# Seven products in every w2 step, sums that stay in PSUM over a pass boundary, and the residual parked in DRAM

## The chip, the cores and the metric

The kernel runs on one core of one Trainium2 chip. The metric is device time in microseconds: the median of three runs of the kernel before is 1998.59 (1996.66 to 1999.63). The engines are named as in the profile: TensorE is PE (its weight loads PEld), VectorE is DVE, ScalarE is ACT, SyncE is SP, whose queue issues nearly all DMA transfers.

## The reference

256 positions of 2048 channels go through two layers, everything in float32. Layer 0 mixes by a gated short convolution, layer 1 by latent attention with 16 heads; each mixer is followed by a squared-ReLU feed-forward part of 8192 hidden channels, and each of these four sub-layers by a layer norm of `ALPHA * x + f(x)`.

```python
def short_conv_mixer(x, w_in, conv_w, w_out):
    gate_b, gate_c, u = jnp.split(x @ w_in, 3, axis=-1)
    y = conv3(gate_c * u, conv_w)              # causal, width 3, per channel
    return (gate_b * y) @ w_out

def sq_relu_mlp(x, w1, w2):
    return jnp.square(jax.nn.relu(x @ w1)) @ w2

# layer 0: mix = short_conv_mixer(h); layer 1: mix = mla_mixer(h)
h = layer_norm(ALPHA * h + mix, ...)
h = layer_norm(ALPHA * h + sq_relu_mlp(h, w1, w2), ...)
```

## The kernel before

**Arithmetic.** Every float32 operand is split into a rounded part `hi` and a rest `lo` (`split`, L125: ScalarE casts, VectorE subtracts), and a product is three matmuls: hi·hi, hi·lo, lo·hi. Weights are split on the chip as they arrive.

**The weight stream.** `stream` (L78) lists all weight blocks of 128 × 1024 in the order of use. `take` (L183) hands out the next block and runs `prepare` (L141) for blocks up to `LOOK` = 5 steps ahead: a load on SP's queue into one of `RAW` = 5 raw buffers, the cast by ScalarE and the subtraction by VectorE into one of `WA` = 8 pairs of hi and lo tiles. A raw buffer is free when VectorE has read it, a hi or lo tile when TensorE has. The compiler's scheduler puts the instructions of each engine into one fixed order, which may differ from the order of the Python text; at run time each engine goes through its list in that order and waits for semaphores.

**The feed-forward part** (`mlp`, L575) is used twice, as part 1 after the convolution (profile from about 362 to 1057 us) and as part 3 after the attention (from about 1304 us on). It goes through eight passes q over 1024 hidden channels each (eight chunks of 128). In a pass the w1 products come first: eight chunks m, each 32 matmuls of TensorE (`products`, L288), evacuated by `whole` (L352; ScalarE copies a half, VectorE adds), then relu and square on ScalarE (`hidden`, L713). Then come the w2 products.

**Passes 1 to 6** (`FAST`) use Strassen-like sums for w2. Positions are cut into two halves, the 2048 output columns into four blocks of 512, two column blocks making a group g. For a pair j of hidden chunks and a group, seven products of 128 × 512 (`FACTORS`, L340) replace eight. They need sums S1 to S4 of the activations (`form`, L703, into the tile `forms`) and differences T1 to T4 of the weights, made by VectorE in three steps of `prepare`: block r1 is split; T1 and T3 are computed and split; T2 and T4 are computed and split with r2. `MIXED = "sssp"` says that in the first group (g = 1) three pairs go by seven products and the fourth ("p") by the eight plain dots; the second group (g = 0) takes seven products for all four pairs. One plain matmul is cut into two halves (`EVEN`).

**Sums.** Each of the seven products, and an eighth bank for the plain pair, is summed over pairs in a PSUM bank and over passes in SBUF: in `sums` (for products 1, 5, 7 and 6) or in `acc`. `resumed` copies a sum into its bank (ScalarE), `put_back` copies it out (ScalarE), `keep` adds it to what lies in SBUF (VectorE). `fold` (L669) makes the output blocks out of the sums in pass 7. Four banks serve the w1 products, four hold sums.

**The residual** lies in `xres` (2 MB) all the time. In part 1 `begin` runs `Norm.prepare` on its 16 chunks, chunk 0 in pass 0 and the others in pass 7. In part 3 `extra` (`turn_residual`, L1024) transposes it on TensorE and adds it into `acc`, a quarter in each of the passes 1 to 4.

Of the kernel before, what the change touches and what calls it, by code (L numbers as in the profile page):

```python
# [16 lines left out]
P = 128  # L17
W = 256 + 2
T = 256
# [14 lines left out]
RAW, WA = 5, 8  # L34
# [3 lines left out]
MIXED = "sssp"  # L38
EVEN = (QC - 1, "22")
# [7 lines left out]
WO_G = 3  # L47
BEHIND = (2, 2, 2, 3, 2, 2, 3)
# [5 lines left out]
def trunk(ctx: ExitStack, tc: tile.TileContext, xT, vecs, lead, w_first, w_in, w_out, w_kv, w_q, w_uk, w_uv,  # L54
# [12 lines left out]
    xres = act.tile([P, NC, T], F32, tag="xres", name="xres")  # L67
    for tag, columns in (("c", 4096), ("a2", 4128), ("a1", 4128), ("b", 8256)):
        act.tile([P, columns], F32, tag=tag, name=f"at_{tag}")
# [7 lines left out]

    stream = []  # L78
# [20 lines left out]
    stream += halves(w_o) + mlp_stream(1)  # L99

# [40 lines left out]
    def prepare(i):  # L141
# [7 lines left out]
        r1, r2 = (load_raw(f"{i}_{j}", src) for j, src in enumerate(stream[i]))  # L149
        out = []  # L150

        def finished(r, name):
# [3 lines left out]

        b22, (b21, b12) = r1[:, BW:], (r2[:, :BW], r2[:, BW:])
# [12 lines left out]
        f = state["fast"].tile([P, 2, BW], F32R, tag="t4", name=f"t4_{i}", bufs=2)  # L170
        split(f[:, 0, :], f[:, 1, :], t4)
        b1, t13, b2 = ([[v.rearrange("p b c -> p (b c)")[:, o:o + BW] for v in w] for o in (0, BW)] for w in out)
        ready[i] = {"11": b1[0], "22": b1[1], "21": b2[0], "T2": b2[1], "T1": t13[0], "T3": t13[1],
                    "T4": [f[:, 0, :], f[:, 1, :]]}
# [168 lines left out]
    def fast_products(ps, x, forms, j, fresh, ready, onto=()):  # L343

        b, = take(1)
        a = {"11": held(x[2 * j], 0), "12": held(x[2 * j + 1], 0), "22": held(x[2 * j + 1], 1)}
        for i in range(4):
            a[f"S{i + 1}"] = [forms[:, j, o, i * P:(i + 1) * P] for o in range(2)]
        for p, l, r in FACTORS:
            dot(ps[p], b[r], a[l], p in fresh, p in ready, onto=p in onto)  # L350

# [40 lines left out]
    class Norm:  # L392
# [10 lines left out]
        def prepare(self, m, bank=None):  # L403

            d = xres[:, m, :]
# [11 lines left out]
        def count(self, m):  # L417
            d = xres[:, m, :]
# [21 lines left out]
        def wide(self, m):  # L440
            d, x, g = xres[:, m, :], self.xd[m], self.gain(m)[0]
# [31 lines left out]
        def normal(self, m, dst=None):  # L473

            g, b = self.gain(m)
            d = xres[:, m, :]
# [22 lines left out]
    def add(ps, m):  # L499
        d = xres[:, m, :]  # L500
        nc.vector.tensor_tensor(d, d, ps[:, :T], ALU.add)

    def summed(ln, pss, add, m0=0):

        for m, ps in enumerate(pss, m0):
            add(ps, m)
            ln.count(m)
            ln.wide(m)
# [38 lines left out]
    ln = Norm(0, ALPHA)  # L547
    for m in range(NC):
# [19 lines left out]
        if m >= NC // 2:  # L568
            for k in range(2 * m - NC, 2 * m - NC + 2):
                ln.prepare(k)  # L570
    nc.sync.dma_start(id_t, ident)
    ln.widen("a1", "a2")
    summed(ln, chain(products(1, z), lagged(NC - 1, z)), residual)

    def mlp(idx, ln, blocks, fast, begin=None, extra=None, last=False):  # L575
# [25 lines left out]
        sums = fast.tile([P, 4, 2, BW], F32, name=f"sums{idx}")  # L601

        def place(p, g):

            return sums[:, OWN.index(p), g, :] if p in OWN else \
                block(*{"2": (2 * g, 0), "3": (2 * g + 1, 0), "4": (2 * g, 1), "22": (2 * g + 1, 1)}[p])

        def resumed(p, g, name, bank):

            ps = psum(name, bank)  # L610
            if q != FAST[0] or p not in OWN:
# [3 lines left out]
        def put_back(p, g, ps):  # L615
            nc.scalar.copy(place(p, g), ps)

        def keep(p, g, ps):

            at = place(p, g)  # L620
            if q == FAST[0] and p in OWN:
# [4 lines left out]
        def resume(busy, free, ps, m):  # L626

            b2, b3, b4, b6 = free
            b1, b5, b7, b22 = busy
            for p, bank in {3: (("3", b3),), 4: (("2", b2),), 5: (("4", b4), ("1", b1)), 6: (("6", b6), ("5", b5)),  # L630
                            7: (("7", b7), ("22", b22))}.get(m, ()):
                ps[p] = resumed(p, 1, f"ps_r{p}", bank)

        def down_pairs(h, forms, busy, free, ps):

            b2, b3, b4, b6 = free
            b1, b5, b7, b22 = busy
            new = set(OWN) if q == FAST[0] else set()
            onto = set(ps) - new
            for j, kind in enumerate(MIXED):  # L640
                if kind == "s":
                    last = j == MIXED.rindex("s")
                    fast_products(ps, h, forms, j, new if j == 0 else (), OWN if last else (), onto)
                    if last:
                        for p in OWN:
                            put_back(p, 1, ps[p])
                        then = {p: resumed(p, 0, f"ps_f{p}", bank) for p, bank in (("3", b1), ("1", b5))}
                    continue
                for two in (((0, "2"), (1, "4")), ((1, "22"), (0, "3"))):
                    w, = take(1, LOOK + 1)  # L650
                    for t, p in two:
                        for kk in range(2):
                            k = 2 * j + kk
                            dot(ps[p], wide_rows(w, kk), held(h[k], t), False, k == QC - 1, (k, p) == EVEN, True)
                    if j == len(MIXED) - 1:
                        if "5" not in then:
                            then.update({p: resumed(p, 0, f"ps_f{p}", bank) for p, bank in (("5", b7), ("7", b6))})
                        for _, p in two:
                            put_back(p, 1, ps[p])
            n = QC // 2  # L660
            onto = set(then) - new
            then.update({p: psum(f"ps_f{p}", bank) for p, bank in (("2", b2), ("6", b4), ("4", b22))})
            for j in range(n):
                fast_products(then, h, forms, j, set(then) - onto if j == 0 else (), then if j == n - 1 else (), onto)
            for p, _, _ in FACTORS:
                (put_back if p in onto or p in new else keep)(p, 0, then[p])
            return (b3, b1, b5, b7), (b6, b2, b4, b22)

        def fold():  # L669
# [3 lines left out]
            for d, a, b in ((c[:, 0, 0], c[:, 0, 0], s1), (s6, s6, s1), (c[:, 0, 1], c[:, 0, 1], s6), (s7, s7, s6),  # L673
                            (c[:, 1, 0], c[:, 1, 0], s7), (c[:, 1, 1], c[:, 1, 1], s7),
                            (c[:, 0, 1], c[:, 0, 1], s5), (c[:, 1, 1], c[:, 1, 1], s5)):
# [10 lines left out]
        busy, free = (0, 1, 2, 3), (4, 5, 6, 7)  # L686
        for q in range(NQ):
            ht = act.tile([P, QC, 2 * T], F32R, tag="c", name=f"h{idx}_{q}")
            h = [ht[:, k, :] for k in range(QC)]
            forms = None  # L690
# [497 lines left out]
```

## Time and profile before

| | us |
|---|---|
| median of three runs | 1998.59 (1996.66 to 1999.63) |
| span of the profiled execution | 1994.9 |
| what lies between that span and the median | 3.7 |
| PE busy | 1987.7 (100% of the span) |
| PEld busy | 1737.2 (87%) |
| DVE busy | 1709.4 (86%) |
| ACT busy | 1354.9 (68%) |
| one pass of part 1, for example 619.23 to 702.46 | 83.23 |

Of the profiled execution the span, from its first to its last instruction, is what the profile gives as its own time. Matmuls are pipelined: the busy time of one (0.39 us at 512 columns) overlaps the next, so a busy PE is no proof that it never waits; the distance from start to start tells more. The same holds on a smaller scale for DVE. The granted TensorE clock is 1.00 throughout, so no stretch is slowed by the clock.

### The profile page before, as it was taken

The page shows a single profiled execution, that of the slowest core. Times are in us where ns is not written, and L with a number is a line of the kernel's source. Part 1 is how long each engine was busy: PE and PEld are TensorE (multiplying, and loading weights), DVE is VectorE, ACT ScalarE, POOL GpSimd, SP SyncE. Part 2 cuts the span into 40 slices and gives each one's busy share as a digit, 9 for nine tenths or more (in the row PEclk, how much of TensorE's full clock was granted, in tenths as well). Part 3 has the DMA queues.
Part 4 walks back from the last instruction along what each step waited for, and adds up shares of the span by engine and source line. Part 5 has one row for each costly group of instructions (what it writes and reads, how often), then busy time and mean ns, then how long its engine had stood idle before and what let it go on. Part 6 is the DMA issues. An engine that isn't in the chain of part 4 may idle for free.

```text
span 1994.9 us, 30180 instructions
## 1 busy us (share of the span) xinstructions
PE 1987.7 (100%) x11110; PEld 1737.2 (87%) x11110; DVE 1709.4 (86%) x2555; ACT 1354.9 (68%) x2154; POOL 2.3 (0%) x21
## 2 busy tenths in 40 slices
PE   9999999999999999999999999999999999999998
PEld 8888888988888888888889998898888888888886
DVE  8667667797999989989978988777899999999985
ACT  6444445586778778777756755558677787887772
POOL 0000000000000000000000000000000000000000
PEclk9999999999999999999999999999999999999999
DMA  8666666565657466574855543656464656656483
GB/s 318 205 191 187 190 190 190 179 193 157 212 170 251 148 216 221 177 243 147 281 171 159 170 140 123 201 180 195 146 233 155 232 161 220 222 178 233 150 269 130
DMA packets 106853, 385.85 MB, mean 193 GB/s; under 512 B 11857, under 2 KB 12625, under 8 KB 106449
## 3 DMA queue, kind: packets, MB, share of 16 engines
q1 hardware_dynamic: 106560, 383.79, 59.5%
q8 instruction: 87, 1.43, 0.3%
q14 instruction: 62, 0.50, 0.1%
q10 hardware_dynamic: 144, 0.13, 0.0%
HBM read 381.78 MB, written 2.10 MB: 192 GB/s over the span
## 4 chain that ended last, share of the span: by engine, by line
PE 98%; DVE 1%; ACT 1%; issue 0%; DVEq 0%; ACTq 0%
PE ps_u L215 20%; PE ps_l L215 13%; PE ps_u L219 10%; PE ps_l L219 7%; PE ps_f L300 4%; PE ps_f L303 4%; PE ps_f L302 4%; PE ps_r L303 4%; PE ps_r L302 4%; PE ps_r L300 4%; PE ps_d L300 2%; PE ps_d L302 2%; PE ps_d L303 2%; PE ps_w L249 2%; PE ps_w L248 2%; PE ps_w L247 2%
## 5 line engine op out<-in xcount | busy, mean ns | idle before, releaser
L128 DVE TENSOR_TENSOR lo<-raw,hi 128x1024 fp32r<-128x1024 f32 x710 | 861.8, 1220 | 190.6 <-ACT hi L127 119.9
L127 ACT CAST hi<-raw 128x1024 fp32r<-128x1024 f32 x710 | 741.8, 1051 | 247.4 <-PE ps_l L215 98.1
L215 PE MATMUL ps_u<-xhl,hi 128*128 128x512 f32 x1792 | 621.7, 392 | 0.0
L219 PE MATMUL ps_u<-xhl,lo 128*128 128x256 f32 x1792 | 498.2, 279 | 0.0
L215 PEld LDWEIGHTS ps_u<-xhl,hi 128*128 128x128 f32 x1792 | 334.5, 187 | 73.6 <-ACT acc L595 0.2
L219 PEld LDWEIGHTS ps_u<-xhl,lo 128*128 128x128 f32 x1792 | 338.1, 189 | 1.8
L215 PE MATMUL ps_l<-xhl_a,hi 128*128 128x512 f32 x704 | 244.1, 393 | 0.0
L219 PE MATMUL ps_l<-xhl_a,lo 128*128 128x256 f32 x704 | 195.4, 279 | 0.0
L215 PEld LDWEIGHTS ps_l<-xhl_a,hi 128*128 128x128 f32 x704 | 132.1, 188 | 29.9
L219 PEld LDWEIGHTS ps_l<-xhl_a,lo 128*128 128x128 f32 x704 | 131.9, 188 | 0.2
L127 ACT CAST hi_t<-raw_t 128x1024 fp32r<-128x1024 f32 x84 | 88.5, 1054 | 45.8 <-DVE raw_t L162 41.4
L162 DVE TENSOR_TENSOR raw_t<-raw,raw 128x1024 f32<-128x1024 f32 x84 | 102.3, 1218 | 1.8 <-DMA raw<-in_w2f_dram 1.5
L128 DVE TENSOR_TENSOR lo_t<-raw_t,hi_t 128x1024 fp32r<-128x1024 f32 x84 | 102.4, 1219 | 0.2
L718 ACT ACTIVATE fp<-fp 128x256 f32<-128x256 f32 x96 | 40.0, 416 | 63.2 <-DVE fp L356 62.6
L215 PE MATMUL ps_l<-z,hi 128*128 128x512 f32 x240 | 82.4, 391 | 0.0
L300 PE MATMUL ps_d<-hi,h 128*128 128x512 f32 x192 | 75.0, 391 | 0.0
L302 PE MATMUL ps_d<-lo,h 128*128 128x512 f32 x192 | 75.0, 390 | 0.0
L303 PE MATMUL ps_d<-hi,h 128*128 128x512 f32 x192 | 74.8, 389 | 0.0
L249 PE MATMUL ps_w<-xd,hi 128*128 128x258 f32 x256 | 72.7, 284 | 0.0
L248 PE MATMUL ps_w<-xd,lo 128*128 128x258 f32 x256 | 72.3, 282 | 0.0
L247 PE MATMUL ps_w<-xd,hi 128*128 128x258 f32 x256 | 72.3, 282 | 0.0
L215 PE MATMUL ps_l<-oT,hi 128*128 128x512 f32 x208 | 71.3, 391 | 0.0
(296 smaller groups left out, 3963.7 us busy)
## 6 DMA issues: line engine op xcount, KB each, us to landing
raw<-in_w_dram SPq DMA_DIRECT2D x344, 512.0 KB, 4.5
raw<-in_w2f_dram SPq DMA_DIRECT2D x168, 512.0 KB, 3.9
raw<-in_w_in_dram SPq DMA_DIRECT2D x88, 512.0 KB, 4.2
raw<-in_w_out_dram SPq DMA_DIRECT2D x32, 512.0 KB, 3.7
raw<-in_w_o_dram SPq DMA_DIRECT2D x32, 512.0 KB, 4.2
raw<-in_w_kv_dram SPq DMA_DIRECT2D x10, 512.0 KB, 3.7
raw<-in_w_q_dram SPq DMA_DIRECT2D x8, 512.0 KB, 4.0
raw<-in_w_uk_dram SPq DMA_DIRECT2D x8, 512.0 KB, 3.9
```

Of the source, the lines that this page charges most:

```text
L127: nc.scalar.copy(hi, src)
L128: nc.vector.tensor_tensor(lo, src, hi.bitcast(F32), ALU.subtract)
L162: nc.vector.tensor_tensor(t.rearrange(two, a=2), b12.unsqueeze(1).to_broadcast([P, 2, BW]), r1.rearrange(two, a=2), ALU.subtract)
L215: nc.tensor.matmul(ps, w[blk // 8][0][:, blk % 8, :], x, start=first, stop=False)
L219: nc.tensor.matmul(ps[:, :T], w[blk // 8][1][:, blk % 8, :], x[:, :T], start=False, stop=last)
L247: nc.tensor.matmul(ps[:, :W], hi, x[k][:, :W], start=k == 0, stop=False)
L248: nc.tensor.matmul(ps[:, :W], lo, x[k][:, :W], start=False, stop=False)
L249: nc.tensor.matmul(ps[:, :W], hi, x[k][:, W:], start=False, stop=k == NC - 1)
L300: nc.tensor.matmul(ps, x[0], w[0], start=first, stop=False, skip_group_check=onto)
L302: nc.tensor.matmul(ps[:, at], x[0], w[1][:, at], start=False, stop=False, skip_group_check=onto)
L303: nc.tensor.matmul(ps, x[1], w[0], start=False, stop=last, skip_group_check=onto)
L718: nc.scalar.activation(f, f, AF.Relu)
```

## The change

It has five parts.

1. **Seven products throughout.** `MIXED` and `EVEN` go. Both groups take seven products for all four pairs of a pass.
2. **Alternating groups.** Pass 1 takes the groups in the order (1, 0), pass 2 (0, 1), and so on, so that the last group of a pass is the first of the next. The sums of the products 3, 1, 5 and 7 of that group stay in their banks over the w1 products of the next pass (`stay`); the sums of 2, 6 and 4 are copied out at the end and in again in the next pass (`first_sums`). At the change of groups, in the last pair of the first group, each product's sum is copied out as soon as its last matmul is done and the next product's sum of the other group is copied into its bank (`turn`, called through `then`). All of these copies are ScalarE's; VectorE's additions (`keep` into SBUF) go.
3. **The residual in DRAM.** In part 1 `begin` runs in pass 1 for all chunks, each two chunks are stored to `parked` by SP's queue, and `sums` takes over the place of `xres`. In pass 7 four loads bring it back as `xback`. In part 3 `extra` turns all four quarters in pass 1.
4. **Deeper ring.** `RAW` goes from 5 to 7, `WA` from 8 to 9.
5. **One row.** Activations and sums of a pair lie in one row `u` of eight blocks of 128 columns: relu and square run once over 512 columns, three VectorE instructions instead of four make S1 to S4, and one split of 896 columns writes all seven left factors.

`EARLY` and `FRESH` are empty, so `making`, `made` and the branch of `prepare` for four sources do nothing here and are left out below.

```diff
-RAW, WA = 5, 8
+RAW, WA = 7, 9
-MIXED = "sssp"
-EVEN = (QC - 1, "22")
...
+    def groups(q):
+        return (1, 0) if (q - FAST[0]) % 2 == 0 else (0, 1)
...
-            for j, kind in enumerate(MIXED):
-                out += [(w2f[l, q, 1, j, 0], w2f[l, q, 1, j, 1])] if kind == "s" else \
-                    halves(w2[l, q, 2, j]) + halves(w2[l, q, 3, j])
-            out += [(w2f[l, q, 0, j, 0], w2f[l, q, 0, j, 1]) for j in range(QC // 2)]
+            for i, g in enumerate(groups(q)):
+                for j in range(QC // 2):
+                    out.append((w2f[l, q, g, j, 0], w2f[l, q, g, j, 1]) + made.get((l, q, i, j), ()))
...
+    LEFT = ("11", "22", "12", "S1", "S3", "S2", "S4")
+    def fast_products(ps, x, j, fresh, ready, onto=(), then=None):
         b, = take(1)
+        a = {n: [x[j // 2][:, j % 2, o, i * P:(i + 1) * P] for o in range(2)] for i, n in enumerate(LEFT)}
         for p, l, r in FACTORS:
             dot(ps[p], b[r], a[l], p in fresh, p in ready, onto=p in onto)
+            if then:
+                then(p)
...
+        def first_sums(ps, banks, m):
+            g = groups(q)[0]
+            for p in {3: ("3", "1", "5", "7") if q == FAST[0] else (), 4: "2", 5: "6", 6: "4"}.get(m, ()):
+                banks.setdefault(p, busy[m % 4])
+                ps[p] = begun_sum(p, g, f"ps_r{p}", banks[p])
...
+            def turn(p):
+                keep(p, first, ps[p], max(q - 1, FAST[0]) if p in order[:4] else q)
+                i = order.index(p) + 1
+                if i < len(order):
+                    begin_next(order[i], banks[p])
+            def end(p):
+                if p not in stay:
+                    keep(p, second, after[p], q)
...
+            for j in range(n):
+                if j == n - 1:
+                    begin_next(order[0], spare)
+                fast_products(ps, h, j, new - held_on if j == 0 else (), ps if j == n - 1 else (),
+                              set(ps) - (new - held_on), turn if j == n - 1 else None)
+            for j in range(n):
+                fast_products(after, h, j, new if j == 0 else (), after if j == n - 1 else (),
+                              set(order) - new, end if j == n - 1 else None)
...
+            def form(j, u):
+                a21, a11, a12, s1, s2, s4 = (u[:, i * P:(i + 1) * P] for i in (0, 1, 3, 4, 6, 7))
+                two = u.rearrange("p (i c) -> p i c", c=P)
+                nc.vector.tensor_tensor(s1, a21, u[:, 2 * P:3 * P], ALU.add)
+                nc.vector.tensor_tensor(two[:, 5:7, :], two[:, 0:5:4, :], a11.unsqueeze(1).to_broadcast([P, 2, P]),
+                                        ALU.subtract)
+                nc.vector.tensor_tensor(s4, a12, s2, ALU.subtract)
+                f = factors[j // 2][:, j % 2]
+                split(f[:, 0, :], f[:, 1, :], u[:, P:])
...
                 for m, ps in enumerate(products(QC, xhl, TURNED, busy)):
                     hidden(m, ps, whole)
-                    if extra and m == 0 and q <= NB:
+                    if extra and q == FAST[0] and m < NB:
                         for t in range(2):
-                            extra(block, q - 1, t, busy[2 + t])
+                            extra(block, m, t, busy[2 + t])
+                    if begin and q == FAST[0]:
+                        begin(range(max(2 * m, 1), 2 * m + 2))
+                        nc.sync.dma_start(parked[:, 2 * m:2 * m + 2, :], held_x[0][:, 2 * m:2 * m + 2, :])
+                    if q == FAST[0] and m == QC - 1:
+                        sums = act.tile([P, 4, 2, BW], F32, tag="xres", name=f"sums{idx}")
...
-                        if begin:
-                            begin(range(max(2 * m, 1), 2 * m + 2))
+                if begin and q == NQ - 1:
+                    held_x[0] = act.tile([P, NC, T], F32, tag="xres", name="xback")
+                    for k in range(0, NC, 4):
+                        nc.sync.dma_start(held_x[0][:, k:k + 4, :], parked[:, k:k + 4, :])
```

More of the change, by code (lines that the diff above doesn't have):

```diff
@@ L169, in prepare @@
         nc.vector.tensor_tensor(t4, b21, b12, ALU.subtract)
[L170 to L174, printed above, removed]
+        ready[i] = {**named((("11", "22"), ("T1", "T3"), ("21", "T2"))), "T4": fourth(t4)}
         yield
@@ L570, in trunk @@
                 ln.prepare(k)
+        if m >= MAKE_FROM:
+            next(before_mlp, None)
     nc.sync.dma_start(id_t, ident)
     ln.widen("a1", "a2")
-    summed(ln, chain(products(1, z), lagged(NC - 1, z)), residual)
+    summed(ln, chain(products(1, z), lagged(NC - 1, z)), residual, maker=before_mlp)
+    making_in.close()
     def mlp(idx, ln, blocks, fast, begin=None, extra=None, last=False):
@@ L710, in form @@
                 nc.vector.tensor_tensor(s4, a12, s2, ALU.subtract)
-                split(forms[:, j, 0, :], forms[:, j, 1, :], sf.rearrange("p i c -> p (i c)"))
+                f = factors[j // 2][:, j % 2]
+                split(f[:, 0, :], f[:, 1, :], u[:, P:])
             def hidden(m, ps, evac, *func):
-                both = pair_tile(m) if q in FAST else None
-                f = both[:, m % 2, :] if both is not None else tmp.tile([P, T], F32, tag="fh", name="fh", bufs=3)
+                if q in FAST:
+                    if m % 2 == 0:
+                        pair.append(fast.tile([P, 8 * P], F32, tag="fp", name="fp"))
+                    u = pair[-1]
+                    evac(ps, u[:, (m % 2) * T:(m % 2 + 1) * T])
+                    if m % 2:
+                        for function in (AF.Relu, AF.Square):
+                            nc.scalar.activation(u[:, :2 * T], u[:, :2 * T], function)
+                        form(m // 2, u)
+                    return
```

183 lines of the change are left out of this document (95 added, 88 removed).

## The prediction

> **What bounds the kernel now.** I read the page first, then stretches of one pass of the feed-forward part (tables of busy time by stretch), then the instructions at the end of a pass in order of time, and last the groups and waits of the engines that feed TensorE.
>
> ```profile
> span 1994.9 us, 30180 instructions
> PE 1987.7 (100%) x11110; PEld 1737.2 (87%) x11110; DVE 1709.4 (86%) x2555; ACT 1354.9 (68%) x2154; POOL 2.3 (0%) x21
> PE 98%; DVE 1%; ACT 1%; issue 0%; DVEq 0%; ACTq 0%
> ```
>
> By the page TensorE is the bound. The twelve fast passes (q = 1 to 6 of both feed-forward parts) show how near the next engine is. Columns: stretch in us, its length, then busy us of PE, PEld, DVE, ACT, POOL.
>
> ```profile
> 452.78:536.00 83.22, 83.22 (x429) 71.27 (x428) 72.44 (x96) 59.25 (x92) 0.00 (x0) 1.00 0.52 161
> 536.00:619.23 83.23, 83.23 (x429) 71.28 (x428) 78.12 (x101) 66.47 (x104) 0.00 (x0) 1.00 0.60 199
> 619.23:702.46 83.23, 83.23 (x430) 71.27 (x428) 80.16 (x104) 67.44 (x103) 0.00 (x0) 1.00 0.64 207
> 702.46:785.68 83.22, 83.22 (x429) 71.28 (x428) 78.12 (x101) 65.41 (x103) 0.00 (x0) 1.00 0.59 197
> 785.68:868.91 83.23, 83.23 (x429) 71.28 (x428) 79.66 (x104) 66.73 (x102) 0.00 (x0) 1.00 0.62 205
> 868.91:953.06 84.15, 83.69 (x429) 71.12 (x428) 78.52 (x102) 66.34 (x103) 0.00 (x0) 1.00 0.59 198
> 1394.56:1478.65 84.09, 84.09 (x438) 71.89 (x436) 73.90 (x98) 58.95 (x90) 0.00 (x0) 1.00 0.52 158
> 1478.65:1562.74 84.09, 84.09 (x437) 71.87 (x436) 79.64 (x104) 67.02 (x105) 0.00 (x0) 1.00 0.60 200
> ...
> 1814.15:1897.38 83.23, 83.23 (x429) 71.28 (x428) 78.53 (x101) 65.72 (x103) 0.00 (x0) 1.00 0.58 200
> 619.23:663.62 44.39, 44.39 (x257) 39.12 (x256) 41.67 (x58) 35.59 (x57) 0.00 (x0) 1.00 0.72 235
> 663.62:702.46 38.84, 38.84 (x175) 32.15 (x173) 38.49 (x47) 31.86 (x46) 0.00 (x0) 1.00 0.55 174
> ```
>
> A pass takes 83.23 us almost to the hundredth, so TensorE sets it; but VectorE is busy for 78.1 to 80.2 of it. The last two rows split one pass: 44.39 us of w1 products (VectorE 41.67 busy), then 38.84 us of w2 products, in which VectorE has no rest (38.49). It cannot keep up there and lives on weights prepared before. The end of that stretch shows what is left:
>
> ```profile
> 696.01 1.22 DVE L128 TENSOR_TENSOR lo_t<-raw_t,hi_t 128x1024 fp32r<-128x1024 f32 x1
> 697.15 1.22 DVE L128 TENSOR_TENSOR lo<-raw,hi 128x1024 fp32r<-128x1024 f32 x1
> 698.29 0.69 DVE L128 TENSOR_TENSOR t<-raw,t 128x512 fp32r<-128x512 f32 x1
> 698.89 2.35 DVE L128 TENSOR_TENSOR lo<-raw,hi 128x1024 fp32r<-128x1024 f32 x2
> ...
> 699.06 0.39 PE L300 MATMUL ps_f<-hi_t,forms 128*128 128x512 f32 x1
> 699.28 0.39 PE L302 MATMUL ps_f<-lo_t,forms 128*128 128x512 f32 x1
> 699.51 0.39 PE L303 MATMUL ps_f<-hi_t,forms 128*128 128x512 f32 x1
> ```
>
> The last pair's T1/T3 tile is done at 697.23 (696.01 + 1.22) and first read at 699.28: 2 us of reserve. Starts also give the true prices: 0.227 us per 512-column matmul (699.51 − 699.06, halved), 1.14 us per 1024-column VectorE instruction, 0.60 per 512-column one; the durations beside them overlap. The pass from 868.91 is 0.92 us longer than its fellows; in it the chain of waits runs through VectorE and ScalarE and ends with a sum copy that TensorE waits for:
>
> ```profile
> 936.91 0.52 ACT t L127
> 937.43 0.49 ACT acc L616
> 937.97 0.50 PE ps_f L300
> ```
>
> The Trainium skill (Perfetto Trace Analysis, Identifying the Most-Contended Engine) says matmul busy time does not tell the bound; weight-load busy time and the other engines' occupancy do. By it VectorE (99% of 663.62:702.46, weight loads 83%) is the contended engine of the second half, and TensorE time saved there would be worth nothing: VectorE's added 1.2 us a pass (below) would then be the whole effect, 10 × 1.2 = +12 us. The trace agrees half: 99% busy, yet no matmul late.
>
> **The change, part by part.**
>
> ```profile
> L128 DVE TENSOR_TENSOR lo<-raw,hi 128x1024 fp32r<-128x1024 f32 x33 | 40.1, 1220 | 2.5 <-ACT hi L127 2.3
> L162 DVE TENSOR_TENSOR raw_t<-raw,raw 128x1024 f32<-128x1024 f32 x7 | 8.5, 1218 | 0.2 <-DMA raw<-in_w2f_dram 0.2
> L166 DVE TENSOR_TENSOR raw<-raw,raw_t 128x512 f32<-128x512 f32 x7 | 4.8, 687 | 0.1
> L356 DVE TENSOR_TENSOR fp<-ps_u,t 128x256 f32<-128x256 f32 x8 | 3.3, 418 | 0.0
> L709 DVE TENSOR_TENSOR sf<-sf,fp 128x128 f32<-128x128 f32 x4 | 1.2, 291 | 0.1
> L624 DVE TENSOR_TENSOR acc<-acc,ps_f 128x512 f32<-128x512 f32 x3 | 2.0, 683 | 0.1
> ```
>
> (groups of the pass 619.23:702.46)
>
> *TensorE.* The one plain pair of a pass took 8 dots, 25 matmuls, one of them in two halves: 24 × 512 columns. A seven-product pair takes 21. Saved: 3 × 0.227 = 0.68 us a pass. A pass needs 82.55 us; if nothing stalls, 12 × 0.68 + 0.92 = 9.1 us are won. That is the ceiling, 1990.
>
> *VectorE.* A seven-product pair in place of the plain one adds one T1/T3 difference and one split (2 × 1.14 = 2.28) and three 512-column ones (1.8). Gone are the additions of L624 (34 in 12 passes, 2.8 × 0.60 = 1.7) and eight 512-column splits of h and forms (4.8); in their place four splits of 896 columns (between 0.60 and 1.14, taken as 1.00: 4.0). The four 128-column form instructions become two and one of 256; started back to back these are 0.08 shorter than 291 and 418 ns, so 8 × 0.2 less and 4 × 0.33 more: −0.3. Sum 2.28 + 1.8 − 1.7 − 4.8 + 4.0 − 0.3 = +1.3; from the compiled list +1.2, which I take. VectorE goes from 79.0 (mean of the six rows from 536.00 to 1562.74 that are not first passes) to 80.2 us, in 82.55.
>
> *The rings (RAW 7, WA 9).* A pair wants 4 × 1.14 + 3 × 0.60 = 6.4 us of VectorE and lasts 21 × 0.227 = 4.77 us. Eight pairs: 51 us against 38.2, so 13 must be ready ahead; before, 7 pairs and the plain one with the additions: 48.6 against 38.8, so 10. The ninth tile is worth about 2.1 us (a third of a pair). So the ring makes up most of the deficit, not all: reserve 2 − 1 = about 1 us at the best pass, none at others. The longer raw ring removes waits for loads, a part of the 2.5 us of idle time in the first row of groups.
>
> *ScalarE at the change of groups.* Before, eight sums were put back over a seven-product pair and the plain one:
>
> ```profile
> 674.74 0.59 ACT L616 COPY sums<-ps_r 128x512 f32<-128x512 f32 x1 [2.50 <-PE ps_r L303]
> 675.27 1.05 ACT L127 CAST hi_t<-raw_t 128x1024 fp32r<-128x1024 f32 x1
> 677.69 1.55 ACT L616 COPY sums<-ps_r 128x512 f32<-128x512 f32 x3
> 682.06 1.13 ACT L612 COPY ps_f<-sums 128x512 f32<-128x512 f32 x2
> ...
> ACT fp L718 <- DVE fp L356: 31.7, 28, 2.6
> ```
>
> Now one pair (4.77 us) ends all seven: 7 copies out and 6 in, 13 × 0.52 (674.74 to 675.27) = 6.8 us, with one cast between them in the compiled order. Casts behind them are late by 2 to 5 us, and VectorE's splits need the casts. Price: 0 (VectorE has other work) to 3 us a pass; I take 0.2 beyond the old waits, since the old order also held casts behind copies and VectorE still was 38.49 busy. The Trainium skill (TensorE: Matmul & The Clock Gate, Architectural detail) calls ScalarE and VectorE strict first-in, first-out. If so a cast can't pass the copies and the price is the upper end, 10 × 3 = 30 us; if casts could pass it is 0. The row of 674.74 (idle 2.50, the cast right behind) agrees, but shows no VectorE loss.
>
> Likewise relu and square now wait for both chunks of a pair, and one row is used in turn: ScalarE waited 31.7 us in 28 waits for VectorE there (L718, in the stretch 1400:1900). Fewer, later waits: −1 to +1 us a pass, taken as 0. In the compiled order VectorE prepares nine w1 tiles ahead of its work on the second chunk of a pass, where it prepared eleven: nine take 10.3 us, the two chunks 11.1 (44.39 / 4), so it may idle there for up to 1 us.
>
> *Banks over the pass boundary* save no copies (240 against 236 of ScalarE, and VectorE's 34 additions): 0.
>
> *The residual.* In the first part's pass 1: 16 prepare instructions (L415) come from pass 7, and eight 256 KB stores and four 512 KB loads go onto SP's queue.
>
> ```profile
> L415 DVE SCALAR_TENSOR_TENSOR xres<-xres,mu 128x256 f32<-128x256 f32 x45 | 16.6, 418 | 0.0
> SPq L138 <- DVE lo L128: 874.6, 368, 16.2
> out_dram<-acc SPq DMA_DIRECT2D x8, 256.0 KB, 2.4
> raw<-in_w_out_dram SPq DMA_DIRECT2D x32, 512.0 KB, 3.7
> ```
>
> 16 × 0.33 = 5.4 us of VectorE, in a pass with 10.8 idle (72.44 of 83.22): hidden. Behind a waiting store the next weight load waits; SP waits for VectorE's splits anyway (874.6 us). Without that cover it is 8 × 2.4 = 19 us, once. The loads go in pass 7 behind the last fold, 4 × 3.7 = 15 us if all in line, needed two column blocks (22 us) later: 0. In the second part the turning of the residual (84.09 − 83.23 = 0.86 us in each of four passes) moves into pass 1, 3.5 us in all; its banks are handed on at once, so TensorE may wait up to four times 1 us for VectorE: 1 us.
>
> **Sum.** Twelve passes before: 953.06 − 452.78 + 1897.38 − 1394.56 = 1003.1 us. After: first passes 82.55 and 82.55 + 3.5 + 1 = 87.0; the ten others as long as VectorE needs, 80.2 plus its idle time. That was 3.1 to 5.6 us before, mean 4.5 over the same six rows (5.11, 3.07, 5.11, 3.57, 5.63, 4.45). With 4.5 + 0.2: 84.9, but the deeper raw ring gives some of it back; I take 84.6, 0.3 less. 846 + 169.5 − 1003.1 = +12.4. The profiled span 1994.9 lies 3.7 below the median of 1998.59: 1994.9 + 12.4 + 3.7 = 2011.
>
> **Rivals.**
> - *The rings hide it.* VectorE's idle time falls to 2.3 to 2.8 us and a pass takes 82.55 to 83.0 us: 4 to 9 us won, 1990 to 1995. For it: idle time includes waits for a full ring, which cost nothing, and 3.07 was enough once. Against it: that pass kept only 2 us of reserve with a smaller deficit. Below 83.4 us a pass (833.6 + 169.5 = 1003.1) the kernel is faster than before.
> - *A tie.* Passes of 83.0 to 83.8: within 4 us.
> - *ScalarE's burst becomes the bound.* Each change of groups costs 3 us more: passes of 86 to 87.5, 2025 to 2040. For it: 6.8 us of copies in 4.77. Against: they end before TensorE needs the banks.
> - *Nothing is done.* Excluded: the list has 48 matmuls fewer.
>
> **How the numbers follow.** 0.2% is 4 us, what repeated runs can tell. Forecast (83.8 to 86 us a pass, 2003 to 2025) 0.58; burst 0.06; tie 0.12, rings 0.24. Range 1990 to 2025; the forecast's own is 2003 to 2025. Faster 0.24, same 0.12, slower 0.64.
>
> **What would show it.** Right: passes 2 to 6 of 84 us or more, VectorE above 80 us in each, and TensorE waiting for lo_t near the end of the second group; about 48 matmuls less; pass 1 near 82.6. Wrong: passes of 82.55 with VectorE idle 2 us. The weakest step is that VectorE's idle time stays as it was.

## The result and the profile after

The changed kernel takes 2022.62 us (median, 2022.02 to 2023.62); the kernel before, run beside it, 1998.57 (1996.66 to 1999.63). The ratio is 1.012 with a 95% interval of 1.0105 to 1.0134: slower by 24 us. The profiled execution has a span of 2021.0 us, 26.1 more than before.

The page of the changed kernel (span; busy time by engine; the chain that ended last, by engine):

```profile
span 2021.0 us, 29789 instructions
...
PE 2002.4 (99%) x11062; PEld 1726.4 (85%) x11062; DVE 1727.7 (85%) x2485; ACT 1332.7 (66%) x1998; POOL 2.3 (0%) x21
...
PE 73%; DVE 15%; ACT 8%; issue 5%; DMA 0%; DVEq 0%; ACTq 0%; SPq 0%
```

48 matmuls are gone, yet the span grew. The chain of waits was 98% TensorE's before; now 15% of it runs through VectorE and 8% through ScalarE. The stretches (columns as in the prediction: stretch, its length, then busy PE, PEld, DVE, ACT, POOL, clock, DMA share, GB/s) of both first passes, of the passes 2 to 6 of each part taken together, and of the two halves of one pass:

```profile
452.95:539.16 86.21, 84.46 (x426) 70.08 (x424) 72.29 (x89) 56.20 (x79) 0.00 (x0) 1.00 0.49 146
539.16:965.74 426.58, 421.88 (x2122) 351.48 (x2120) 403.21 (x482) 322.49 (x443) 0.00 (x0) 1.00 0.62 198
1409.30:1496.87 87.57, 87.11 (x458) 73.75 (x456) 77.16 (x97) 56.50 (x78) 0.00 (x0) 1.00 0.46 138
1496.87:1922.77 425.90, 421.10 (x2122) 351.16 (x2121) 403.31 (x482) 322.82 (x443) 0.00 (x0) 1.00 0.61 198
...
624.07:669.14 45.07, 45.07 (x256) 39.15 (x256) 41.58 (x52) 33.30 (x45) 0.00 (x0) 1.00 0.69 234
669.14:709.49 40.35, 39.40 (x171) 31.20 (x170) 39.01 (x46) 31.09 (x44) 0.00 (x0) 1.00 0.50 156
...
1753.33:1838.05 84.72, 83.76 (x425) 70.11 (x424) 80.67 (x97) 64.48 (x89) 0.00 (x0) 1.00 0.60 199
```

(the last row is a pass of part 3) and the passes 2 to 6 of the kernel before:

```profile
536.00:953.06 417.06, 416.61 (x2141) 356.22 (x2140) 394.58 (x508) 332.41 (x511) 0.00 (x0) 1.00 0.61 201
...
1478.65:1897.38 418.73, 418.73 (x2165) 358.17 (x2164) 397.39 (x514) 333.05 (x512) 0.00 (x0) 1.00 0.60 201
```

The ten passes went from 835.79 to 852.48 us (83.58 to 85.25 each), the two first passes from 167.31 to 173.78. That is 23.2 of the 26.1 us; the other 2.9 lie outside the twelve passes, 1.4 of them in the w1 products of the last pass of each part, 45.1 us each where 44.39 are needed. VectorE's work went from 79.20 to 80.65 us a pass and its idle time from 4.38 to 4.60.

These w1 products got slower without a wait on record and at a granted clock of 1.00, and so did those inside most passes: in 624.07:669.14 two of them (512 and 256 columns) follow the two before after 0.353 us (six such pairs from 639.83 to 641.95), where the kernel before needs 0.347 (639.70 to 641.78). Seven of the ten passes show it and take 85.41 to 85.63 us; the three that don't take 84.91, 84.72 and 84.72. So some 0.7 us of those seven passes, and of the two last w1 halves, is neither VectorE's work nor a wait that the trace names. In no_t4 and early_2 (below) none of the ten passes shows it. What causes it was not found.

Where the time goes is seen at the end of a pass. The chain of waits there (start, us, what):

```profile
779.55 1.10 ACT hi L159
...
780.68 0.04 DVE lo L160
...
788.25 1.15 DVE raw_t L216
...
789.42 0.02 ACT hi_t L159
789.44 0.93 issue
790.37 1.05 ACT hi L159
...
791.47 1.02 PE ps_f L350 x3
```

From 780.68 VectorE works without a break; the T1/T3 difference of the last pair is finished only at 789.40, ScalarE casts it and then the next block, and TensorE starts on that block 0.05 us after the cast. Nothing is ready ahead any more.

### The profile page after: what moved, and what is told of

The parts are those of the page before. It is cut to its first block, busy times and chain, and to the rows that moved or that the text cites. A ratio compares the mean times of both kernels' runs of the same rounds, so it can differ in the third digit from the quotient of the medians.

```text
span 2021.0 us, 29789 instructions
## 1 busy us (share of the span) xinstructions
PE 2002.4 (99%) x11062; PEld 1726.4 (85%) x11062; DVE 1727.7 (85%) x2485; ACT 1332.7 (66%) x1998; POOL 2.3 (0%) x21
## 4 chain that ended last, share of the span: by engine, by line
PE 73%; DVE 15%; ACT 8%; issue 5%; DMA 0%; DVEq 0%; ACTq 0%; SPq 0%
PE ps_u L265 18%; PE ps_l L265 13%; PE ps_u L269 9%; PE ps_l L269 7%; DVE lo L160 5%; ACT hi L159 3%; DVE raw_t L216 3%; PE ps_d L350 2%; PE ps_d L353 2%; PE ps_d L352 2%; ACT ps_f L682 2%; DVE t L160 1%; DVE lo_t L160 1%; PE ps_w L299 1%; PE ps_w L297 1%
## 5 line engine op out<-in xcount | busy, mean ns | idle before, releaser
L265 PE MATMUL ps_u<-xhl,hi 128*128 128x512 f32 x1792 | 629.8, 396 | 0.2 <-DVE acc L1091 0.2
L159 ACT CAST hi_t<-raw_t 128x1024 fp32r<-128x1024 f32 x96 | 101.4, 1057 | 85.6 <-DVE raw_t L216 80.6
L216 DVE TENSOR_TENSOR raw_t<-raw,raw 128x1024 f32<-128x1024 f32 x96 | 116.8, 1217 | 8.6 <-DMA raw<-in_w2f_dram 8.2
L160 DVE TENSOR_TENSOR lo_t<-raw_t,hi_t 128x1024 fp32r<-128x1024 f32 x96 | 117.0, 1218 | 1.0 <-ACT hi_t L159 1.0
L159 ACT CAST t<-raw 128x512 fp32r<-128x512 f32 x96 | 59.8, 623 | 48.4 <-DVE raw L223 40.0
L407 ACT COPY t<-ps_u 128x256 f32<-128x256 f32 x112 | 41.2, 368 | 62.8 <-PE ps_u L269 62.6
L299 PE MATMUL ps_w<-xd,hi 128*128 128x258 f32 x256 | 72.8, 284 | 0.0
```

Of the source, the lines that this page charges most:

```text
L159: nc.scalar.copy(hi, src)
L160: nc.vector.tensor_tensor(lo, src, hi.bitcast(F32), ALU.subtract)
L216: nc.vector.tensor_tensor(t.rearrange(two, a=2), b12.unsqueeze(1).to_broadcast([P, 2, BW]), r1.rearrange(two, a=2), ALU.subtract)
L265: nc.tensor.matmul(ps, w[blk // 8][0][:, blk % 8, :], x, start=first, stop=False)
L299: nc.tensor.matmul(ps[:, :W], hi, x[k][:, W:], start=False, stop=k == NC - 1)
L407: nc.scalar.copy(t, ps[:, T:])
```

## Experiments

The table gives for each run the whole time (with that of the kernel before on the same chip), and for passes 2 to 6 of part 1, taken as one stretch and divided by five, the length, VectorE's busy time and the rest. Of the experiments pool_t4, early_1 and early_2 were run four times, the others once; runs of the kernel before on one chip differ by about 4 us. TensorE alone needs 82.55 us.

| kernel | whole | before beside it | pass | VectorE | idle |
|---|---|---|---|---|---|
| before | 1998.57 | | 83.41 | 78.92 | 4.50 |
| changed | 2022.62 | 1998.57 | 85.32 | 80.64 | 4.67 |
| no_t4 | 1994.47 | 1996.22 | 82.71 | 75.20 | 7.51 |
| no_copy_in | 2003.07 | 1996.22 | 83.28 | 79.90 | 3.38 |
| no_turn_in | 2009.71 | 2000.02 | 83.85 | 80.32 | 3.53 |
| ring_7_8 | 2029.91 | 1996.22 | 86.20 | 80.58 | 5.62 |
| ring_5_10 | 2026.82 | 1996.22 | 85.99 | 80.69 | 5.30 |
| ring_5_8 | 2041.85 | 2000.02 | 87.30 | 81.19 | 6.11 |
| before_ssss | 2051.74 | 1999.76 | 88.63 | 83.60 | 5.03 |
| no_park | 2022.46 | 1999.76 | 85.47 | 80.71 | 4.76 |
| pool_t4 | 2071.37 | 1999.76 | 89.59 | 82.99 | 6.60 |
| pool_t13 | 2126.30 | 1999.76 | 94.58 | 84.70 | 9.88 |
| early_1 | 2051.26 | 2000.02 | 84.17 | 78.17 | 6.00 |
| early_2 | 2098.72 | 2000.02 | 82.71 | 75.68 | 7.03 |

### Less work for VectorE

```diff
-        nc.vector.tensor_tensor(t4, b21, b12, ALU.subtract)
```

> The changed kernel without the subtraction that makes T4 (the split takes the unsubtracted block, so the fourth product is not the reference's). It takes 8 x 0.60 = 4.8 us of VectorE out of each fast pass and nothing else. Theory 'VectorE and the rings' (TensorE waits because VectorE cannot make the weights of the w2 half in time from what the rings hold ready): the passes of 85.42 us fall to the 82.55 that TensorE needs, or to within 0.3 of it, the first pass of part 1 from 86.21 by at least 2, the whole to 1986 to 1992. Rival 'ScalarE's burst' (the 13 copies at the change of groups hold the casts back): the copies are as before, the passes stay at 84.5 or more, the whole above 2010.

The first pass and the passes 2 to 6 of part 1:

```profile
452.78:537.03 84.25, 83.55 (x425) 70.36 (x424) 69.08 (x83) 57.45 (x80) 0.00 (x0) 1.00 0.51 158
537.03:950.60 413.57, 413.47 (x2121) 352.83 (x2120) 376.01 (x440) 320.28 (x442) 0.00 (x0) 1.00 0.62 203
```

With 5.4 us less of VectorE a pass TensorE is the bound again (82.71). So it was waiting for weights. The whole is 2.5 us above the bracket: first passes of 84.25 and 87.25 stay above the floor. The whole is 1.75 us under the kernel before, less than repeated runs differ by, and not the 9.1 of the prediction's ceiling.

### Fewer copies for ScalarE

First all copies into banks left out, then only the six at the change of groups:

```diff
@@ no_copy_in: new_sum, begun_sum
-            return p in FRESH or (q == FAST[0] and p in OWN)
+            return True
...
-            if not new_sum(p):
-                nc.scalar.copy(ps, place(p, g))
@@ no_turn_in: begin_next (and the products after it begin new)
-                after[p], place_of[p] = begun_sum(p, second, f"ps_f{p}", bank), bank
+                after[p], place_of[p] = psum(f"ps_f{p}", bank), bank
```

> The changed kernel with no sum copied into a bank: every product starts its bank anew, so earlier passes' sums are lost and the output is not the reference's. It takes about 9 of 16 sum copies (9 x 0.52 = 4.7 us of ScalarE) out of each fast pass, six of them out of the burst at the change of groups. 'ScalarE's burst': with the burst halved the passes fall from 85.42 to 82.6 to 83.2, the whole to 1988 to 1997. 'VectorE and the rings': only the 0.87 us that VectorE idles behind the burst and a few tenths at the pass boundary can go, passes of 84.2 to 85.2, the whole 2007 to 2019.

> The changed kernel without the copies into the banks at the change of groups alone (six ScalarE copies of 0.52 us in each fast pass; three remain in the w1 half): the second group of a pass starts its sums anew, so the output is not the reference's. Leaving all copies in out took 1.9 us off a pass. If that came from the burst at the change of groups: passes of 83.2 to 84.2, the whole 2001 to 2010. If it came from the three copies in the w1 half: passes of 84.8 to 85.4, the whole 2016 to 2023.

Rows of the passes 2 to 6 of part 1, of the one and of the other:

```profile
539.52:955.94 416.42, 416.04 (x2121) 352.86 (x2120) 399.52 (x480) 295.91 (x391) 0.00 (x0) 1.00 0.62 202
```

```profile
539.03:958.30 419.27, 418.33 (x2122) 352.36 (x2121) 401.60 (x481) 303.04 (x407) 0.00 (x0) 1.00 0.61 201
```

VectorE's work hardly changed (0.7 and 0.3 us less a pass), its idle time fell by 1.3 and 1.1, and the pass by 2.0 and 1.5. So no_copy_in lies between its two theories, and no_turn_in in the bracket of the burst: two thirds to three quarters of what the copies cost comes from those six (1.2 of 1.9 us a pass over all ten passes, 1.5 of 2.0 over these five). They are a part of the cause that I had put too low, at 1.2 us at most. Without any copies in, a pass is no longer than the kernel before's (83.28 against 83.41), with VectorE still at 79.90: the added work of VectorE and the bunched copies are both needed for the slowdown, and either cut takes it away. But the kernel before has such copies too, only spread wider, so this run leaves out more than the change added. ScalarE in order of time at the change of groups of the changed kernel, then VectorE's wait:

```profile
775.10 0.61 ACT L682 COPY ps_f<-sums 128x512 f32<-128x512 f32 x1
775.61 1.07 ACT L159 CAST hi_t<-raw_t 128x1024 fp32r<-128x1024 f32 x1
776.56 0.61 ACT L682 COPY ps_f<-acc 128x512 f32<-128x512 f32 x1
...
779.08 0.62 ACT L689 COPY acc<-ps_r 128x512 f32<-128x512 f32 x1
779.55 1.09 ACT L159 CAST hi<-raw 128x1024 fp32r<-128x1024 f32 x1
```

```profile
779.11 0.69 DVE L220 TENSOR_TENSOR raw<-raw,raw_t 128x512 f32<-128x512 f32 x1
780.68 1.23 DVE L160 TENSOR_TENSOR lo<-raw,hi 128x1024 fp32r<-128x1024 f32 x1 [0.87 <-ACT hi L159]
```

Six copies stand between two casts, and VectorE waits 0.87 us for the second. Over the five passes its waits for casts of `hi` fall from 14.8 to 11.9 us in no_turn_in, and those for ScalarE's evacuations of w1 products (L408) from 5.4 to 3.1, so about half of the idle time saved is not of the kind shown here.

### The rings

```diff
-RAW, WA = 7, 9
+RAW, WA = 7, 8        # ring_7_8; 5, 10 in ring_5_10; 5, 8 in ring_5_8
```

> The changed kernel with 8 pairs of hi and lo tiles instead of 9, raw ring of 7 kept. 'VectorE and the rings': a tile less ready at the start of the w2 half costs what VectorE takes to make one, 6.4 / 3 = 2.1 us a pass: passes of 87.3 to 87.6, the whole 2043 to 2050. Rival 'rate alone' (VectorE's 80.6 us of work and the 4.8 us it idles in evacuations set the pass, whatever the ring holds): passes within 0.5 of 85.4, the whole 2018 to 2028. 'ScalarE's burst': the same as rate alone.

> The changed kernel with 10 pairs of hi and lo tiles instead of 9, for which the raw ring goes back from 7 to 5 (the memory allows no more). 'VectorE and the rings', if the hi and lo tiles are what counts: a tile more is worth 2.1 us a pass: passes of 83.2 to 83.5, the whole 1995 to 2001. If the raw buffers count too, two fewer of them take some of it back: passes of 83.5 to 85.4, the whole 2000 to 2023. 'Rate alone' or 'ScalarE's burst': passes of 85.4 or more, the whole 2022 or more.

> The changed kernel with the rings of before (5 raw buffers, 8 pairs of hi and lo tiles). One tile less cost 0.95 us a pass (2029.9), and two raw buffers less took away more than what a tenth tile gave (2026.8). If both add up: passes of 87 to 89, the whole 2040 to 2065. If the two rings stand in for each other (either full ring stops the loads): passes of 86 to 87, the whole 2029 to 2040.

ring_7_8, first pass and passes 2 to 6 of part 1:

```profile
453.40:537.59 84.19, 83.53 (x427) 70.33 (x425) 73.32 (x91) 57.38 (x80) 0.00 (x0) 1.00 0.54 164
537.59:968.59 431.00, 425.09 (x2121) 350.81 (x2121) 402.91 (x481) 322.06 (x443) 0.00 (x0) 1.00 0.60 195
```

ring_5_10, the same, and ScalarE's waits in the second stretch (us in total, times, longest):

```profile
452.89:535.46 82.57, 82.57 (x426) 70.61 (x425) 72.27 (x89) 55.99 (x78) 0.00 (x0) 1.00 0.50 153
535.46:965.40 429.94, 423.47 (x2123) 350.62 (x2121) 403.44 (x481) 324.44 (x443) 0.00 (x0) 1.00 0.59 196
```

```profile
ACT hi L159 <- DMA raw<-in_w_dram: 19.4, 36, 1.6
...
ACT hi L159 <- DMA raw<-in_w2f_dram: 8.8, 7, 1.7
```

The same wait of the changed kernel, passes 2 to 6:

```profile
ACT hi L159 <- DMA raw<-in_w_dram: 1.0, 2, 0.8
```

One pair of tiles less costs 0.9 us a pass, not 2.1: VectorE's work stays and its idle time grows by 0.95. Two raw buffers less cost as much (ring_5_8 against ring_7_8: 1.1); ScalarE's casts then wait for loads, 28.2 us in five passes; the first of the two waits is 1.0 in the changed kernel. The effects roughly add up (87.30), as one of the expectations for ring_5_8 had it. For ring_7_8 neither theory gave 86.20, and in ring_5_10 the passes came out where "rate alone" put them (85.99), though its reason, that the rings don't matter, is refuted by the other two runs: the tenth tile was paid for with raw buffers. So a ring is worth the idle time that it saves; the price of making a tile is not its worth.

### The first part of the change alone

```diff
-MIXED = "sssp"
-EVEN = (QC - 1, "22")
...
-            for j, kind in enumerate(MIXED):
...
+            for j in range(n):
+                fast_products(ps, h, forms, j, new if j == 0 else (), ps if j == n - 1 else (), onto)
+            for p, _, _ in FACTORS:
+                put_back(p, 1, ps[p])
```

> The kernel before with the first part of the change alone: the plain pair of the first group goes by seven products too; rings of 5 and 8, two rows, the old order of groups. 'VectorE sets the pass': TensorE needs 82.55 us, but VectorE gets 2.28 + 1.8 = 4.1 us more, 79.0 + 4.1 = 83.1 us and its idle time of 4.5: passes of 87 to 88, the whole 2040 to 2056; so the other parts of the change would have given back about 25 us. Rival 'ScalarE's copies set it' (the copies of before are spread wider, and no burst stands at one pair): passes of 82.6 to 84, the whole 1990 to 2008.

```profile
540.34:983.47 443.13, 427.57 (x2121) 355.77 (x2120) 417.98 (x536) 336.54 (x513) 0.00 (x0) 0.98 0.58 191
```

Seven products throughout cost the kernel before 52 us; VectorE got 4.7 us more a pass, not 4.1, and its 83.6 us exceed what TensorE needs even without idle time. Not all of it is VectorE's: the granted clock is 0.98 in this row, as it stands at 0.50 for some microseconds four times (for example from 802.34 to 804.34); from stretches of 1 us I estimate about 7 us lost by it here and 3 in part 3. The other parts of the change gave 29.1 us back. With the rings of before (ring_5_8) the changed kernel takes 2041.85: the rings gave 19.2 of it, the parts 2, 3 and 5 together 9.9.

### The residual's storing

```diff
-                    if begin and q == FAST[0]:
-                        begin(range(max(2 * m, 1), 2 * m + 2))
-                        nc.sync.dma_start(parked[:, 2 * m:2 * m + 2, :], held_x[0][:, 2 * m:2 * m + 2, :])
...
+                    if begin and n == NB - 1:
+                        for k in range(0, NC, 2):
+                            nc.sync.dma_start(parked[:, k:k + 2, :], held_x[0][:, k:k + 2, :])
```

> The changed kernel without the residual's 15 preparing instructions in pass 1 of the first part, and with its eight stores issued at the end of pass 0, where nothing keeps them waiting (what comes back is the residual unprepared, so the output is not the reference's). If storing the residual is what made that pass 86.21 us where 82.55 was forecast: 82.5 to 83.5, the whole 3 us faster than the changed kernel, 2018 to 2020. If the pass is long for the same reason as the others (51 us of VectorE for the weights of a w2 half that TensorE needs in 38, with nine tiles at most ready): 85.0 to 86.2, the whole 2021 to 2023.

```profile
453.22:539.01 85.79, 84.16 (x425) 70.15 (x424) 72.32 (x89) 56.20 (x79) 0.00 (x0) 1.00 0.48 141
```

The first pass goes from 86.21 to 85.79 only, the whole not at all. So preparing and storing cost nothing, but not in the way that the forecast and this expectation assume: in the changed kernel's compiled order the 15 instructions (L467) run from 434.84 to 447.98 and the eight stores are issued from 435.28 to 450.91, all before the pass begins. VectorE's work in the pass is the same with and without them (72.29 and 72.32 us); the end of pass 0 hid them, and the first pass begins at 452.95 where it began at 452.78 before. The halves of that pass in the changed kernel show what it is instead:

```profile
452.95:497.34 44.39, 44.39 (x257) 39.12 (x256) 31.43 (x42) 27.00 (x38) 0.00 (x0) 1.00 0.43 133
497.34:539.16 41.82, 40.07 (x171) 30.95 (x169) 40.86 (x48) 29.20 (x42) 0.00 (x0) 1.00 0.54 159
```

VectorE rests 13 us in the w1 half and can't use them, then works 40.86 of 41.82 us in the w2 half. The kernel before has the same division:

```profile
452.78:497.17 44.39, 44.39 (x258) 39.12 (x256) 33.93 (x50) 29.15 (x49) 0.00 (x0) 1.00 0.51 150
497.17:536.00 38.83, 38.83 (x174) 32.15 (x173) 38.51 (x47) 30.09 (x43) 0.00 (x0) 1.00 0.53 173
```

With ten tiles (ring_5_10) this pass takes 82.57. But with eight and seven raw buffers it takes 84.19, less than with nine. VectorE's waits in this pass of the changed kernel point to loads:

```profile
DVE raw_t L216 <- DMA raw<-in_w2f_dram: 6.4, 4, 2.6
DVE lo L160 <- ACT hi L159: 6.3, 5, 1.9
```

The first wait is 0.6 us in the kernel before, 1.5 in ring_5_10 and 3.0 in ring_7_8, so late w2 blocks are a likely part of the cause. They are not all of it (ring_5_8: 1.4, and 10.7 for casts, in a pass of 86.56), and no run tests it.

### VectorE's subtractions on GpSimd

```diff
-        nc.vector.tensor_tensor(t4, b21, b12, ALU.subtract)
+        nc.gpsimd.tensor_tensor(t4, b21, b12, ALU.subtract)
```

and in the second kernel, in its place, the subtraction for T1 and T3.

> The changed kernel with the subtraction for T4 (128 x 512) on GpSimd instead of VectorE; it computes the same. 'VectorE sets the pass': 4.8 us less of VectorE a pass, as with the subtraction left out: passes of 82.6 to 83.0, the whole 1993 to 1998, if GpSimd does one in under about 3 us and does not slow VectorE. Rival 'a wait takes its place' (GpSimd is slow, or the T4 split waits for it, or VectorE's instructions get longer beside it): passes of 84 to 88, the whole 2008 to 2055; VectorE's mean for its 1024-column subtractions would then be above 1.22 us or it would wait for GpSimd.

> The changed kernel with the subtraction for T1 and T3 (128 x 1024) on GpSimd instead of VectorE; it computes the same. 8 x 1.14 = 9.1 us less of VectorE a pass, but the T2 difference and two splits wait for it. 'VectorE sets the pass': 82.55 to 83.0, the whole 1991 to 1997. Rival 'a wait takes its place': GpSimd needs several us for one; eight in a w2 half of 38 us at more than 4.8 us each cannot be done in time: passes of 86 to 95, the whole 2030 to 2140.

pool_t4 against before: 1.0354 (1.0337 to 1.0372). Its groups in the passes 2 to 6 of part 1, and one subtraction of GpSimd with two of VectorE in order of time (start, us):

```profile
L160 DVE TENSOR_TENSOR lo<-raw,hi 128x1024 fp32r<-128x1024 f32 x161 | 207.3, 1305 | 25.2 <-ACT hi L159 25.0
...
L223 POOL TENSOR_TENSOR raw<-raw 128x512 f32<-128x512 f32 x40 | 80.1, 2003 | 367.8 <-DVE lo L160 116.1 <-DVE fp L759 94.4 <-issue 70.9
```

```profile
782.12 2.06 POOL L223 TENSOR_TENSOR raw<-raw 128x512 f32<-128x512 f32 x1 [9.19 <-issue]
...
781.82 1.21 DVE L216 TENSOR_TENSOR raw_t<-raw,raw 128x1024 f32<-128x1024 f32 x1
783.02 2.24 DVE L160 TENSOR_TENSOR lo<-raw,hi 128x1024 fp32r<-128x1024 f32 x1
```

GpSimd worked from 782.12 to 784.18 (2.06 us); the subtraction that VectorE began at 783.02 took 2.24 us where the one before it took 1.21. Relieved of eight subtractions a pass, VectorE is busier than in the changed kernel (82.99 us against 80.64, and 75.20 where they are left out). The rival holds, and goes beyond its bracket (89.6 us a pass): most of the loss lies inside VectorE's own instructions, and its idle time grows too, from 4.67 to 6.60. For T1 and T3 it is the same on a larger scale (94.58 us a pass, inside the rival's bracket), 40 instructions of 3.09 us:

```profile
L216 POOL TENSOR_TENSOR raw_t<-raw,raw 128x1024 f32<-128x1024 f32 x40 | 123.5, 3090 | 346.0 <-DMA raw<-in_w2f_dram 238.9 <-DVE h_3c L160 33.3 <-DVE h_4c L160 30.5
```

### Differences made ahead

```diff
-EARLY = {}
+EARLY = {0: [(1, 2)], 1: [(1, 2)]}        # early_2: [(1, 1), (1, 3)] for both
-MAKE_FROM = 6
+MAKE_FROM = 3
...
-            if k != l:
-                continue
...
-            if m % 3 == 0:
+            if m % 1 == 0:
                 next(maker, None)
...
-    before_mlp = making(0, making_in.enter_context(tc.tile_pool(name="making0", bufs=2)))
+    before_mlp = making(0, making_in.enter_context(tc.tile_pool(name="making0", bufs=1)))
```

> The changed kernel with the T differences of one pair of eight in each fast pass of both parts made ahead, between 80 and 360 us, where VectorE has rest, and kept in DRAM; the pass loads them (1.75 MB instead of 1 MB for this pair). It computes the same. 'VectorE sets the pass': 1.14 + 0.60 + 0.60 = 2.3 us of VectorE less in a pass: passes of 82.8 to 83.3, the whole 1993 to 2000. Rival 'a wait takes its place' (the pair takes four raw buffers and four loads where it took three and two, on a queue that already waits; or the stage that makes them gets longer): passes of 84 to 86, or as many us lost before 360, the whole 2005 to 2030.

> The same with two pairs of eight in each fast pass, 24 in all: 4.7 us of VectorE less in a pass, as much as without the T4 subtraction, but with the reference's output. 'VectorE sets the pass': passes of 82.55 to 82.8, the whole 1989 to 1996, faster than the kernel before. Rival 'a wait takes its place': the loads of 1.5 MB more in a pass and the fourth raw buffer hold VectorE up, or making 24 pairs ahead lengthens the stages before 360 us: the whole 2000 to 2030.

Against what I wrote, these two kernels do not compute the reference's output; why was not found. They are used here for their times alone. early_1 against before 1.0255 (1.0239 to 1.0270), early_2 1.0497 (1.0479 to 1.0514). early_2, passes 2 to 6 of part 1, and VectorE's waits before the first of them (40 to 480 us):

```profile
642.82:1056.37 413.55, 413.50 (x2121) 352.50 (x2120) 378.38 (x450) 323.02 (x442) 0.53 (x1) 1.00 0.64 222
```

```profile
DVE m L124 <- DMA m<-in_w2f_dram: 73.4, 11, 8.0
DVE m L124 <- issue: 71.3, 10, 8.5
```

Inside the passes the theory holds: 82.71 us, TensorE's floor, as without T4. But VectorE takes its list in order and stood 145 us before the new subtractions, 73 of them for their blocks and 71 without a cause that the trace shows, and the first pass began 106 us later than in the changed kernel (early_1: 43). In early_1 2.5 us of VectorE's work went and the pass fell by 1.15 only, to 84.17 instead of the 82.8 to 83.3 expected, inside the rival's bracket. Its VectorE at the change of groups shows where the rest went:

```profile
812.64 1.23 DVE L158 TENSOR_TENSOR lo_t<-raw_t,hi_t 128x1024 fp32r<-128x1024 f32 x1
816.60 1.23 DVE L158 TENSOR_TENSOR lo<-raw,hi 128x1024 fp32r<-128x1024 f32 x1 [2.74 <-ACT hi L157]
```

VectorE comes earlier to the burst and waits there, 2.74 us instead of 0.87. With the loss ahead of the first pass both rivals hold, and the whole times (2051.26 and 2098.72) lie beyond their brackets. No version that does the whole work beats the kernel before.

## Why the prediction was right, and where its sum was short

The sign, the mechanism and the range hold: 2011 forecast, 2022.6 measured, within 1990 to 2025 and near its upper end. Of the profiled 26.1 us the sum had 12.4.

- *TensorE saves 0.68 us a pass, not won.* Right: the passes 2 to 6 come near 82.55 only with VectorE's work cut (no_t4, early_2: 82.71).
- *VectorE +1.2 us a pass.* Measured +1.46 over the ten passes (80.65 against 79.20; I had taken 79.0 from six of them). With 0.45 above the forecast 80.2, 4.5 us of the miss.
- *Idle time as it was* (4.5 and 0.2, less 0.3 = 4.4), called the weakest step: 4.60, 2 us of the miss. The sum held, its parts did not, and that is luck. The burst was put at 0.2 and costs 1.2 to 1.5 us a pass (no_turn_in: 84.06 a pass over all ten against 85.25). The longer raw ring was put at 0.3 and is worth about 1.1 (measured with eight tiles), the ninth tile, put at 2.1, is worth 0.9. About 0.5 us of the 4.60 is the slower w1 products (an estimate: 0.7 us in seven of ten passes), which no term had.
- *ScalarE's casts behind the copies.* The rule of the Trainium skill (TensorE: Matmul & The Clock Gate, Architectural detail), by which ScalarE is strictly first-in, first-out, agrees with the rows of 776.56 to 779.55; the upper end of 30 us that I drew from it was over twice the measured 12.9 (2022.62 to 2009.71, one run).
- *First pass of part 1 at TensorE's floor, 82.55.* This is the step that failed: 86.21, 3.7 us of the miss. I had set VectorE's 10.8 idle us of the whole pass against its added work, but they lie in the w1 half; the w2 half has none, here as elsewhere. That the residual's preparing and storing is hidden was right (no_park), though they were hidden in pass 0 and not in this pass. Part 3's first pass: 87.0 forecast, 87.57 measured.
- *Outside the passes: nothing.* 2.9 us, 1.4 of them the slower w1 products.
- *What would show it right:* 48 matmuls fewer, VectorE above 80 us, passes above 84: all seen. The fourth sign, pass 1 near 82.6, did not come (86.21). TensorE waits near the end of the second group, but first for ScalarE's casts of late differences, hi_t and hi, rather than for lo_t.
- *The rivals.* "The rings hide it" was answered by ring_7_8 and ring_5_8: the rings give 19 us and are needed, but not enough. "ScalarE's burst" is a real part, not the bound: with it gone passes still take 83.85, and its 12.9 us fall short of the 30 that this rival needs.

By the rule of the Trainium skill (Perfetto Trace Analysis, Identifying the Most-Contended Engine), cited in the prediction, VectorE's +1.2 was to be the whole effect, +12 us. It named the right engine, and measured was twice that: of the profiled 26.1 us the ten passes have 16.7, the two first passes 6.5 and the rest of the program 2.9.

## What to carry to other kernels

When a second engine is 99% busy in one half of a loop, cost the change in that half: its rest in the other half counts only as far as the rings can store it. A burst on an in-order engine takes up what is freed ahead of it (early_1), so work removed before the burst is worth less than its length (2.5 us bought 1.15); whether the same work removed behind it is worth more was not run. And a ring's worth is the idle time it removes, to be read from the waits, not the time to make one more tile.

## What the runs showed of the hardware

GpSimd is no free helper for VectorE here: a 128 × 512 subtraction of float32 took 2.00 us on it on the mean (1.28 to 3.40 over the whole run) against 0.69 on VectorE, and VectorE's 1024-column subtraction beside it 2.24 instead of 1.21. The Trainium skill (SBUF — State Buffer, Who interferes with whom) says that a VectorE instruction with two SBUF inputs contends with a GpSimd instruction that reads SBUF; the trace agrees (2.24 against 1.21).

A long wait of TensorE cost more than itself here. In pool_t4 it waited 3.80 us for a bank, and the seven matmuls from 788.83 to 791.39 started 0.43 us apart instead of 0.227 (rows of 0.63 us instead of 0.39), which is another 1.2 us over these six distances. The granted clock is 0.52 from 788.24 to 791.76, and 1.00 again from 792 to 800. The waits of TensorE in the changed kernel's passes 2 to 6 of part 1 are at most 0.7 us long, and the clock there is 1.00.

```profile
788.24 0.79 PE L350 MATMUL ps_f<-hi,h_4c 128*128 128x512 f32 x1 [3.80 <-ACT ps_f L682]
788.83 0.63 PE L352 MATMUL ps_f<-lo,h_4c 128*128 128x512 f32 x1
...
791.39 0.54 PE L352 MATMUL ps_f<-lo_t,h_4c 128*128 128x512 f32 x1
```
